# Expert-choice encoder layer: the next expert's rows picked and gathered at an earlier place, and the first expert's choice in another order

## The chip, the cores and the metric

The kernel runs on one NeuronCore of a Trainium2 chip. The metric is the device time of one launch in microseconds. Engines in the profile: PE is TensorE, PEld its weight loads, DVE VectorE, ACT ScalarE, POOL GpSimd, SP SyncE. Two queues of DMA matter here: plain loads and stores that SP issues, and the indirect ones (gather and scatter by row index) that POOL issues.

## The reference

One transformer layer, applied with the same weights to a request of 512 tokens (prompt) and one of 2048 tokens (sample), all float32, width 1024:

```
h = x + W_out @ concat[DiffAttn(n), BandGQA(n)],   n = RMSNorm(x)
y = h + ExpertChoiceSwiGLU(RMSNorm(h))

aff = softmax(xt @ w_router)                 # 16 experts
gates, idx = top_k(aff.T, C)                 # C = 2 T / 16: 256 sample rows, 64 prompt rows
xe = xt[idx]
h  = silu(xe @ w_gate[e]) * (xe @ w_up[e])
ye = (h @ w_down[e]) * gates
y.at[idx].add(ye)
```

Each expert picks its rows, so every one of the 16 experts handles 320 rows (256 of the sample, 64 of the prompt).

## The kernel before, in words

The first 1600 us compute projections, attention and the output projection. The output projection runs over 20 blocks of 128 tokens (0 to 15 sample, 16 to 19 prompt). In block b, `outproj` makes the two halves of h, `norm2` (L1411) stores h and its normalised rows, and the block before is transposed (`split_n`, L1388) and given its router logits and softmax (`router`, `router_2`). Work that doesn't belong to the projection is hung in with `at(t, f)` and fires on the t-th `tick`, of which there are about 18 in a block. In the blocks 17 to 19 this carries `choose`, the search for the first expert's threshold, a step at each `slot()` (places in `SLOTS`, L1470); its last steps write the one-hots of the chosen rows (`onehot_s`, L1308) and `pick` the rows.

`pick` (L1315) multiplies the one-hots with row numbers and gates on TensorE (L1329), copies the result (L1332), makes the indices `idx` (L1333) and gates (L1334) on DVE, and then issues three gathers on POOL (L1342): two of 128 sample rows from `n2s_d`, one of 128 rows (the 64 prompt rows twice) from `n2p_d`, 4 KB a row.

Then come the experts, e = 0 to 15. The float32 products run as three fp32r products of high and low parts, so every weight chunk (128 x 2048) is loaded by SP (`w_load`), split into high (ACT, L160) and low (DVE, L161) parts (`w_split`), and used two steps later. `gate_up` has 8 steps f; each makes 24 matmuls for the gate half, then calls `mid()`, then 24 for the up half. In `mid` the kernel does its side work in this order: the split of sums, the weight split and next load, the one-hots of the next expert y (f = 0), and its `pick` (f = 1 from expert 3 on, f = 2 for expert 2). From f = 4 on, `turn` transposes the gathered rows of y, two of eight steps in each f, the first in `mid` of f = 4 (L1584): this needs all three gathers.

From expert 2 on `down_blocks` (L1671) makes the down projection and ends with the scatters, which add into the output in DRAM (L1810): the second sample group `ys[1]`, the prompt rows in two halves into the same rows of `out_p` (`scatter_p`, so that the second half waits until the first has landed), and the first sample group `ys[0]`. POOL runs its instructions in order, so the gathers of the next `pick` stand behind these four. On POOL there are then only the three small sums per f from f = 4 on (L1636 to L1638).

Of the kernel before, what the change touches and what calls it, by code (L numbers as in the profile page):

```python
# [23 lines left out]
NB = NS + NP  # L24
T = NB * P
HEADS = 4
E = 16
# [80 lines left out]
def hybrid_encoder_kernel(tc, a, out_s, out_p):  # L108
# [11 lines left out]
    with ctx:  # L120
# [54 lines left out]
        with ExitStack() as st:  # L175
# [160 lines left out]
            Z, R, X = {}, {}, {}  # L336
# [1023 lines left out]
        with ExitStack() as st:  # L1360
# [106 lines left out]
                    split_wo_l(1, h, k, nc.vector)  # L1467
            split_w(wrh[:, :, 0, :], wrh[:, :, 1, :], wrr)

            SLOTS = (2, 7, 12, 17), (4, 9, 14), (1, 6, 11, 14, 16, 17)  # L1470
            gens = []

            def slot():
                if gens:
                    try:
                        next(gens[0])
                    except StopIteration:
                        gens.pop(0)
# [4 lines left out]
            for b in range(NB):  # L1483
                if b + 2 < NB:
                    MX[b + 2] = load_mx(b + 2)
                if b + 1 < NB:
                    load_res(b + 1)
                if b == 0:
                    for j in range(HEADS * NP):
                        at(14 + 18 * j, lambda j=j: Prompt(0, j // NP, j % NP).start())  # L1490
                    for h in range(2, HEADS):
                        at(72 * h - 50, load_prompt, h)
                if b == NS + 1:
                    rest.close()
                    wsp = pool(ctx, "wsE", 3, side="right")
                if b >= 1:
                    if slow(b - 1):
                        at(12, split_n, b - 1)
                    t = 15 if slow(b - 1) else 13
                    at(t, router, b - 1)  # L1500
                    at(t + 2, router_2, b - 1)
                    if b < NS:
                        at(t + 7, router_3, b - 1)
                    if b == NS:
                        gens.append(first_sample(X[0]))
                        parts = gate_parts(affs, auxs, NS, "s")
                        at(17, router_3, b - 1)
                        at(17, slot)
                if b > NS:
                    at(1, router_3, b - 2) if b > NS + 1 else None  # L1510
                    for t in SLOTS[b - NS - 1]:
                        at(t, slot)
                    at(9, next, parts, None)
                    at(14, next, parts, None)
                if b == 2:
                    at(3, places, auxs, NS)
                    at(9, places, auxp, NP)
                if NS < b < NB - 1:
                    for i in range(4):
                        at(1 + 4 * i, w_split, i)  # L1520
                if b == 0:
                    tick(8)
                else:
                    outproj(b, 0)
                if b >= 1 and not slow(b - 1):
                    split_n(b - 1)
                tick(1)
                if b + 1 < NB:
                    MT[b + 1] = split_m(MX[b + 1])
                tick(1)  # L1530
                outproj(b, 1)
                norm2(b)
                if b == 1:
                    w_load()
                    w_load()
            while gens:
                slot()

        stay.close()

# [6 lines left out]
        with ExitStack() as st:  # L1547
# [123 lines left out]
            def down_blocks(x):  # L1671
# [69 lines left out]
                p = bank("gu1")  # L1741
                product(p, 5, "22b")
                added(y[2][1], q, 2, y[2][1])
                scatter_p(x, x.ys[2])
                added(y[0][1], p, 0, y[0][1])
                scatter(x.idx[:, 0:1], x.ys[0], out_s)
                w_split()
                w_load()

# [64 lines left out]
                for gi in range(2):  # L1814
                    scatter(x.idx[:, gi:gi + 1], x.ys[gi], out_s)

            def scatter_p(x, y):
                for hf in range(2):
                    scatter(x.idx[:CP, 2:3], y[hf * CP:(hf + 1) * CP, :], out_p)

            def last_block(x, y):
# [69 lines left out]
            for e in range(1, E):  # L1891
# [10 lines left out]
                for f in range(FC):  # L1902
                    def mid():
                        if y is not None and f >= 4:
                            turn(y, 2 * (f - 4))
                        if e < 2:
                            w_split()
                            w_load()
                        else:
                            if f:  # L1910
                                split_sums(x, f - 1)
                            if f < 6:
                                w_split()
                            else:
                                split_block(x, ("11", "21")[f - 6])
                            if f < 4:
                                w_load()
                        if y is not None and f == 0:
                            onehot_s(y)
                            onehot_p(y)  # L1920
                        if y is not None and f == (1 if e > 2 else 2):
                            pick(y, 0, 3)
                            if e == 2:
                                scatter_p(X[0], X[0].yp)
                        for n in {3: ("11",), 4: ("12", "22"), 5: ("21",)}.get(f, ()) if e >= 2 else ():
                            load_block(x, n)
# [67 lines left out]
```

## Time and profile before

| | |
|---|---|
| time, median of 3 runs | 3185.86 us (3182.30 to 3187.32) |
| the profiled execution | 3189.75 us, its span 3188.0 us |
| TensorE busy | 3045.8 us, 96% |
| VectorE, ScalarE, GpSimd busy | 2349.1, 1680.5, 1208.9 us |
| mean granted clock of TensorE | 0.989 |
| DMA | 448.26 MB, 141 GB/s over the span |

An expert takes about 88 us from expert 3 on. A row of a timeline gives an instruction's start and length, and the idle time of its engine just before it with what ended that idle time. "Landing" of a DMA is the time from its start on the queue until its completion is seen. Engines other than TensorE idle a good deal; that costs nothing unless TensorE waits for them.

### The profile page before, as it was taken

To read this page: it belongs to the slowest core of one execution; us is meant where nothing else is said; L and a number is where in the kernel's file an instruction comes from. 1 tells how busy PE (TensorE), PEld (TensorE's weight loads), DVE (VectorE), ACT (ScalarE), POOL (GpSimd) and SP (SyncE) were. 2 spreads that over 40 slices of the span, in tenths; PEclk is the share of its full clock that TensorE was granted. 3 is DMA by queue.
4 is the path that set the end of the run, shared out by engine and by line. 5 is a ranking of instruction groups with operands and counts; after the bars stand their busy time and mean duration, and the time that the engine had idled before them with its cause. 6 is when DMAs were issued, how large, how long until landed. Compare 5 with 4: busy or idle time off the path is not lost. (4 is left out here: it accounts for less than half of the span.)

```text
span 3188.0 us, 50336 instructions
## 1 busy us (share of the span) xinstructions
PE 3045.8 (96%) x18996; PEld 2717.8 (85%) x18996; DVE 2349.1 (74%) x4297; ACT 1680.5 (53%) x3199; POOL 1208.9 (38%) x1116
## 2 busy tenths in 40 slices
PE   7998999998999999999997999999999999999997
PEld 5887888886888888888876899999999989999996
DVE  6887777777787788854566656778877767777876
ACT  4333666656777777743333454445555444444553
POOL 3665655554556556632234302122212122222211
PEclk9999999999999999999998999999999999999998
DMA  6664111136030301055533667665555556666553
GB/s 215 179 178 153 57 46 47 56 75 154 22 88 21 87 21 59 28 172 159 156 120 132 196 207 231 198 198 172 177 191 182 192 180 204 212 198 197 170 177 117
DMA packets 169138, 448.26 MB, mean 141 GB/s; under 512 B 15232, under 2 KB 91648, under 8 KB 138560
## 3 DMA queue, kind: packets, MB, share of 16 engines
q1 hardware_dynamic: 152608, 388.68, 37.4%
q0 software_dynamic: 16288, 56.37, 7.7%
q8 instruction: 150, 2.46, 0.3%
q14 instruction: 92, 0.75, 0.1%
HBM read 359.54 MB, written 82.84 MB: 139 GB/s over the span
## 5 line engine op out<-in xcount | busy, mean ns | idle before, releaser
L167 PE MATMUL gu<-xeh,whi 128*128 128x320 f32 (+1 forms) x2048 | 641.8, 313 | 0.0
L169 PE MATMUL gu<-xeh,wlo 128*128 128x320 f32 (+1 forms) x2048 | 631.0, 308 | 0.7 <-DVE wlo L161 0.7
L168 PE MATMUL gu<-xel,whi 128*128 128x320 f32 (+1 forms) x2048 | 630.7, 308 | 0.0
L161 DVE TENSOR_TENSOR wlo<-wraw,whi 128x2048 fp32r<-128x2048 f32 x180 | 412.8, 2296 | 163.5 <-ACT whi L160 163.5
L160 ACT ACTIVATE whi<-wraw 128x2048 fp32r<-128x2048 f32 x180 | 343.2, 1911 | 106.5 <-DMA wraw<-w_gu 50.4
L167 PEld LDWEIGHTS gu<-xeh,whi 128*128 128x128 f32 x2048 | 387.5, 189 | 2.9 <-issue 2.3
L168 PEld LDWEIGHTS gu<-xel,whi 128*128 128x128 f32 x2048 | 386.9, 189 | 0.6
L169 PEld LDWEIGHTS gu<-xeh,wlo 128*128 128x128 f32 x2048 | 386.1, 189 | 0.9 <-DVE wlo L161 0.9
L907 DVE TENSOR_REDUCE cmx<-s 128x1 f32<-128x1024 f32 x256 | 309.4, 1220 | 63.5 <-PE s L895 61.0
L1810 POOL DMA_INDIRECT out_dram<-y,idx x62 | 125.3, 2021 | 582.7 <-DVE y L1692 337.2
L918 ACT ACTIVATE p<-s,cmx 128x1024 f32<-128x1024 f32 x256 | 285.1, 1115 | 81.4 <-DVE cmx L909 78.0
L895 PE MATMUL s<-kd,qd 128*128 128x512 f32 x1024 | 295.3, 416 | 23.8 <-ACT p L918 22.2
L960 PE MATMUL cpo<-vd,aT 128*128 128x128 f32 x2048 | 267.3, 276 | 0.7 <-DVE co L965 0.7
L960 PEld LDWEIGHTS cpo<-vd,aT 128*128 128x128 f32 x2048 | 250.8, 192 | 8.8 <-ACT aT L953 4.6
L167 PE MATMUL z<-w,xh 128*128 128x512 f32 (+1 forms) x624 | 241.1, 386 | 11.7 <-ACT w L163 6.8
L940 POOL TENSOR_SCALAR p<-p,cr 128x1280 f32<-128x1280 f32 (+1 forms) x80 | 144.1, 1802 | 228.6 <-DVE cr L930 190.4
L169 PE MATMUL z<-w,xl 128*128 128x512 f32 (+1 forms) x624 | 229.8, 368 | 0.3 <-POOL xl L692 0.3
L895 PEld LDWEIGHTS s<-kd,qd 128*128 128x128 f32 x1024 | 177.9, 191 | 61.2 <-ACT p L918 35.6
L168 PE MATMUL z<-w,xh 128*128 128x512 f32 (+1 forms) x624 | 229.2, 367 | 0.5 <-DVE w L164 0.5
L953 ACT ACTIVATE aT<-cpt 128x512 f32<-128x512 f32 x272 | 161.8, 595 | 118.3 <-PE cpt L948 114.5
L1636 POOL TENSOR_TENSOR s<-hr,s 128x128 f32<-128x128 f32 x56 | 26.5, 474 | 486.8 <-DVE hr L1604 486.8
L942 POOL TENSOR_TENSOR p<-p,p 128x1280 f32<-128x1280 f32 (+1 forms) x80 | 207.3, 2591 | 6.6
(416 smaller groups left out, 7172.7 us busy)
## 6 DMA issues: line engine op xcount, KB each, us to landing
wraw<-w_gu SPq DMA_DIRECT2D x136, 1024.0 KB, 6.8
b<-w_dn SPq DMA_DIRECT2D x42, 1024.0 KB, 9.1
wraw<-w_dn SPq DMA_DIRECT2D x40, 1024.0 KB, 4.9
xr<-xT SPq DMA_DIRECT2D x40, 512.0 KB, 4.8
kd<-k_d SPq DMA_DIRECT2D x16, 1024.0 KB, 16.5
xtok<-x SPq DMA_DIRECT2D x20, 512.0 KB, 5.0
q_d<-hl SPq DMA_DIRECT2D x20, 512.0 KB, 3.5
k_d<-hl SPq DMA_DIRECT2D x20, 512.0 KB, 3.4
```

What stands on the lines that cost most here:

```text
L160: nc.scalar.activation(hi, raw, AF.Copy)
L161: nc.vector.tensor_sub(lo, raw, hi.bitcast(F32))
L167: nc.tensor.matmul(out, xh, wh, start=start, stop=False)
L168: nc.tensor.matmul(out, xh, wl, start=False, stop=False)
L169: nc.tensor.matmul(out, xl, wh, start=False, stop=stop)
L895: nc.tensor.matmul(s, q, u.keys(c, hl, k0), start=(hl == 0), stop=(hl == 1))
L907: nc.vector.tensor_reduce(m[:, j % 2:j % 2 + 1], u.S[j], axis=AX, op=OP.max)
L918: nc.scalar.activation(u.pr[c][:, half * 1024:(half + 1) * 1024], u.S.pop(j), AF.Exp, bias=u.mx[:, c, 2:], scale=SCALE, accum_out=u.sm[:, ...
L940: nc.gpsimd.tensor_scalar(p1, p1, u.r[:, 1:2], 1.0, op0=OP.mult, op1=OP.mult)
L942: nc.gpsimd.tensor_tensor(p0, p0, p1, op=OP.add)
L953: nc.scalar.activation(u.aT[:, 4 * g:4 * g + 4, :], u.pt, AF.Copy)
L960: nc.tensor.matmul(u.po, u.aT[:, kb, :], u.values(kb), start=(kb == 0), stop=(kb == u.nb - 1))
```

## The change

1. Experts 3 to 14: in `mid` of f = 1, `pick` of the next expert now stands ahead of the weight split and load (in the changed file at L1922). The scatters of the expert before are cut in two: `down_blocks` issues `ys[1]` and the first prompt half; the second prompt half and `ys[0]` (`late_scatters`) are issued only behind that pick's gathers. For the experts 14 and 15 all scatters stay at the end of `down_blocks`.
2. The first expert's choice: the transposes, router and softmax of block 18 leave block 19's projection and come after the pick of the first expert; the last `slot()` of the search, which writes the one-hots, is called after the projection instead of at tick 17.

```diff
@@ -1467,7 +1467,7 @@
                     split_wo_l(1, h, k, nc.vector)
             split_w(wrh[:, :, 0, :], wrh[:, :, 1, :], wrr)
 
-            SLOTS = (2, 7, 12, 17), (4, 9, 14), (1, 6, 11, 14, 16, 17)
+            SLOTS = (2, 7, 12, 17), (4, 9, 14), (1, 6, 11, 14, 16)
             gens = []
 
             def slot():
@@ -1493,7 +1493,7 @@
                 if b == NS + 1:
                     rest.close()
                     wsp = pool(ctx, "wsE", 3, side="right")
-                if b >= 1:
+                if 1 <= b < NB - 1:
                     if slow(b - 1):
                         at(12, split_n, b - 1)
                     t = 15 if slow(b - 1) else 13
@@ -1529,12 +1529,17 @@
                     MT[b + 1] = split_m(MX[b + 1])
                 tick(1)
                 outproj(b, 1)
+                if b == NB - 1:
+                    slot()
                 norm2(b)
                 if b == 1:
                     w_load()
                     w_load()
             while gens:
                 slot()
+            split_n(NB - 2)
+            router(NB - 2)
+            router_2(NB - 2)
 
         stay.close()
 
@@ -1741,9 +1746,10 @@
                 p = bank("gu1")
                 product(p, 5, "22b")
                 added(y[2][1], q, 2, y[2][1])
-                scatter_p(x, x.ys[2])
+                scatter_p(x, x.ys[2], (0,))
                 added(y[0][1], p, 0, y[0][1])
-                scatter(x.idx[:, 0:1], x.ys[0], out_s)
+                if x.e > E - 3:
+                    late_scatters(x)
                 w_split()
                 w_load()
 
@@ -1814,8 +1820,12 @@
                 for gi in range(2):
                     scatter(x.idx[:, gi:gi + 1], x.ys[gi], out_s)
 
-            def scatter_p(x, y):
-                for hf in range(2):
+            def late_scatters(x):
+                scatter_p(x, x.ys[2], (1,))
+                scatter(x.idx[:, 0:1], x.ys[0], out_s)
+
+            def scatter_p(x, y, halves=(0, 1)):
+                for hf in halves:
                     scatter(x.idx[:CP, 2:3], y[hf * CP:(hf + 1) * CP, :], out_p)
 
             def last_block(x, y):
@@ -1909,6 +1919,9 @@
                         else:
                             if f:
                                 split_sums(x, f - 1)
+                            if y is not None and f == 1 and e > 2:
+                                pick(y, 0, 3)
+                                late_scatters(X[e - 1])
                             if f < 6:
                                 w_split()
                             else:
@@ -1918,7 +1931,7 @@
                         if y is not None and f == 0:
                             onehot_s(y)
                             onehot_p(y)
-                        if y is not None and f == (1 if e > 2 else 2):
+                        if y is not None and f == 2 and e <= 2:
                             pick(y, 0, 3)
                             if e == 2:
                                 scatter_p(X[0], X[0].yp)
```

On POOL, at the border of experts 3 and 4 (`y_2151x` are the output rows of expert 3, `xe_` the gathered rows of expert 5), before:

```order
L1810 DMA out_dram<-y_21511,idx 2048x1024
L1810 DMA out_dram<-y_21512,idx 512x1024 x2
L1810 DMA out_dram<-y_21510,idx 2048x1024
L1342 DMA xe_21864<-n2s_d,idx 128x1024
L1342 DMA xe_21866<-n2s_d,idx 128x1024
L1342 DMA xe_21868<-n2p_d,idx 128x1024
L1636 TENSOR_TENSOR s<-hr,s_21702 128x128
```

and now (lines of the changed file are 5 or 6 higher):

```order
L1816 DMA out_dram<-y_21511,idx 2048x1024
L1816 DMA out_dram<-y_21512,idx 512x1024
L1342 DMA xe_21856<-n2s_d,idx 128x1024
L1342 DMA xe_21858<-n2s_d,idx 128x1024
L1342 DMA xe_21860<-n2p_d,idx 128x1024
L1816 DMA out_dram<-y_21512,idx 512x1024
L1816 DMA out_dram<-y_21510,idx 2048x1024
L1641 TENSOR_TENSOR s<-hr,s_21700 128x128
```

The second prompt half and the first sample group have moved behind the three gathers.

On DVE in the half-step f = 1 of expert 4 (`ax`, `idx` and `gate` are the pick's, `wlo` the weight split's low part), before:

```order
L1640 TENSOR_TENSOR hp<-hr,hp 128x64
L161 TENSOR_TENSOR wlo<-wraw,whi 128x2048
L1332 COPY ax<-cnt 128x15
L1333 SCALAR_TENSOR_TENSOR idx<-ax 128x3
L1334 TENSOR_REDUCE gate<-ax 128x3
L1604 TENSOR_TENSOR hr<-hr,gu_21870 128x320
```

and now:

```order
L1645 TENSOR_TENSOR hp<-hr,hp 128x64
L1332 COPY ax<-cnt 128x15
L1333 SCALAR_TENSOR_TENSOR idx<-ax 128x3
L1334 TENSOR_REDUCE gate<-ax 128x3
L161 TENSOR_TENSOR wlo<-wraw,whi 128x2048
L1609 TENSOR_TENSOR hr<-hr,gu_21870 128x320
```

The three instructions of the pick have moved ahead of the split.

On TensorE around the first expert's choice, from the last matmul of the pick on (`pt_1784x` and `pt_1785x` take the transposes of block 19, `n_177xx`; `pt_17886` is the first of the first expert's gathered rows), before:

```order
L1329 MATMUL s<-auxs,wraw 128x5
L1828 MATMUL pt_17848<-ident,n_17775 128x128 x4
L1828 MATMUL pt_17855<-ident,n_17775 128x128 x4
L1459 MATMUL pt<-ident,many 112x128
L1433 MATMUL pt<-xeh,wrh 32x128 x8
L1433 MATMUL pt<-xel,wrh 32x128 x8
L1570 MATMUL pt_17886<-ident,wraw 128x128 x4
```

and now (`n_17599` is block 18):

```order
L1329 MATMUL s<-auxs,wraw 128x5
L1392 MATMUL dpt<-ident,n_17599 128x128 x8
L1433 MATMUL cpo<-nth,wrh 32x128 x8
L1433 MATMUL cpo<-ntl,wrh 32x128 x8
L1442 MATMUL cpo<-ident,lt 128x32
L1838 MATMUL pt_17848<-ident,n_17731 128x128 x4
L1838 MATMUL pt_17855<-ident,n_17731 128x128 x4
L1459 MATMUL pt<-ident,many 112x128
L1433 MATMUL pt<-xeh,wrh 32x128 x8
L1433 MATMUL pt<-xel,wrh 32x128 x8
L1575 MATMUL pt_17886<-ident,wraw 128x128 x4
```

The rows from L1392 to L1442 stood in the last output projection before and now stand in the gap after the pick.

## Rows read from the trace of the kernel before

**Rows 1.** The page, busy time of an engine (share of the span) and its instructions.

```profile
PE 3045.8 (96%) x18996; PEld 2717.8 (85%) x18996; DVE 2349.1 (74%) x4297; ACT 1680.5 (53%) x3199; POOL 1208.9 (38%) x1116
```

**Rows 2.** The waits of TensorE (PE) from 2000 to 3180 us, all lines of the answer: who waited for what: us in total, times, longest.

```profile
PE pt L1584 <- DMA xe<-n2p_d,idx: 17.9, 12, 3.6
PE pt L1584 <- DMA xe<-n2s_d,idx: 1.5, 1, 1.5
```

**Rows 3.** TensorE's timeline at the transposes of the next expert's rows, expert 7 (2410) and expert 9 (2586 to 2594): start us, us, engine, line, operation, times; in brackets the idle time before it and what ended it.

```profile
2410.74 0.33 PE L1584 MATMUL pt<-ident,xe 128*128 128x128 f32 x1 [1.76 <-DMA xe<-n2p_d,idx]
...
2586.41 0.33 PE L1584 MATMUL pt<-ident,xe 128*128 128x128 f32 x1 [1.50 <-DMA xe<-n2s_d,idx]
2590.35 0.48 PE L1584 MATMUL pt<-ident,xe 128*128 128x128 f32 x1 [3.61 <-DMA xe<-n2p_d,idx]
...
2593.56 0.47 PE L169 MATMUL gu<-xeh,wlo 128*128 128x320 f32 x1
```

**Rows 4.** Busy time by stretch (from:to and length in us; PE, PEld, DVE, ACT, POOL busy; then TensorE's granted clock, the DMA engines' mean busy share, GB/s).

```profile
1710.00:1715.00 5.00, 1.66 (x23) 1.57 (x23) 2.30 (x7) 1.15 (x3) 1.20 (x2) 0.50 0.36 140
...
2390.00:2395.00 5.00, 5.00 (x36) 5.00 (x36) 3.63 (x8) 2.22 (x6) 4.31 (x3) 1.00 0.59 90
...
2405.00:2410.00 5.00, 3.98 (x28) 3.74 (x26) 1.12 (x4) 0.66 (x3) 0.00 (x0) 1.00 1.02 423
...
2591.00:2592.00 1.00, 1.00 (x6) 1.00 (x5) 0.64 (x2) 1.00 (x3) 0.00 (x0) 0.50 1.04 434
```

**Rows 5.** POOL's timeline, expert 7 (2379 to 2417) and expert 9 (2573); columns as in rows 3. L1810 is a scatter, L1342 a gather, L1636 the first of the three sums.

```profile
2379.05 2.62 POOL L1810 DMA_INDIRECT out_dram<-y,idx  x1 [0.30 <-issue]
2390.08 1.42 POOL L1810 DMA_INDIRECT out_dram<-y,idx  x1 [8.41 <-DMA out_dram<-y,idx]
2391.81 2.56 POOL L1810 DMA_INDIRECT out_dram<-y,idx  x1 [0.30 <-issue]
2394.67 1.00 POOL L1342 DMA_INDIRECT xe<-n2s_d,idx  x1 [0.30 <-issue]
...
2397.24 2.06 POOL L1342 DMA_INDIRECT xe<-n2p_d,idx  x1 [0.30 <-issue]
2416.67 0.46 POOL L1636 TENSOR_TENSOR s<-hr,s 128x128 f32<-128x128 f32 x1 [17.37 <-DVE hr L1604]
...
2573.30 1.00 POOL L1342 DMA_INDIRECT xe<-n2s_d,idx  x1 [0.30 <-issue]
```

**Rows 6.** The chain of waits, in expert 7 (2397 and 2411) and expert 9 (2575 and 2590): start us, us, what.

```profile
2397.24 13.45 DMA xe<-n2p_d,idx
...
2411.07 0.15 PE gu L167
...
2575.88 14.43 DMA xe<-n2p_d,idx
...
2590.83 0.27 PE gu L167
```

**Rows 7.** Timelines of DVE (VectorE) and, at 2567.33, of ACT (ScalarE): the half-step in which the next expert's rows are picked, expert 7 (2388 to 2393) and expert 9 (2564 to 2569).

```profile
2388.17 0.22 DVE L1640 TENSOR_TENSOR hp<-hr,hp 128x64 fp32r<-128x64 f32 x1
2390.64 2.29 DVE L161 TENSOR_TENSOR wlo<-wraw,whi 128x2048 fp32r<-128x2048 f32 x1 [2.25 <-ACT whi L160]
2392.85 0.17 DVE L1332 COPY ax<-cnt 128x15 f32<-128x15 f32 x1
2393.05 0.16 DVE L1333 SCALAR_TENSOR_TENSOR idx<-ax 128x3 int32<-128x3 f32 x1
...
2564.18 0.21 DVE L1640 TENSOR_TENSOR hp<-hr,hp 128x64 fp32r<-128x64 f32 x1
...
2567.33 1.91 ACT L160 ACTIVATE whi<-wraw 128x2048 fp32r<-128x2048 f32 x1 [3.25 <-DMA wraw<-w_gu]
...
2569.27 2.29 DVE L161 TENSOR_TENSOR wlo<-wraw,whi 128x2048 fp32r<-128x2048 f32 x1 [4.88 <-ACT whi L160]
```

**Rows 8.** TensorE's timeline around the first expert's choice. L1392 are transposes and L1433 router matmuls; L169 is the last matmul of the last output projection, L1828 the last block's transposes, L1570 those of the first expert's gathered rows.

```profile
1696.70 1.03 PE L1392 MATMUL dpt<-ident,n 128*128 128x128 f32 x8
...
1699.76 0.65 PE L1433 MATMUL cpo<-nth,wrh 128*32 128x128 f32 x8
...
1705.00 0.39 PE L169 MATMUL do<-wo,mtl 128*128 128x512 f32 x1
...
1713.85 1.97 PE L1828 MATMUL pt<-ident,n 128*128 128x128 f32 x8 [3.35 <-DVE n L1424]
...
1717.53 1.05 PE L1433 MATMUL pt<-xel,wrh 128*32 128x128 f32 x8
...
1722.85 3.46 PE L1570 MATMUL pt<-ident,wraw 128*128 128x128 f32 x15 [0.80 <-DMA wraw<-n2s_d,idx]
```

**Rows 9.** Timelines of DVE and, at 1714.35, of POOL in the same stretch. L1308 are the one-hots of the first expert, L1409 the addition of the projection, L1424 the last normalisation's product.

```profile
1706.61 3.22 DVE L1308 TENSOR_SCALAR wraw<-iota_s,slots 128x256 bf16<-128x256 bf16 x16
1709.74 0.68 DVE L1409 TENSOR_TENSOR xres<-do,xres 128x512 f32<-128x512 f32 x1
...
1712.51 1.28 DVE L1424 SCALAR_TENSOR_TENSOR n<-xres,dst,ffn_g 128x1024 f32<-128x1024 f32 x1 [0.66 <-POOL dst L155]
...
1714.35 1.11 POOL L1342 DMA_INDIRECT wraw<-n2s_d,idx  x1 [1.88 <-DVE fold L1867]
```

**Rows 10.** The page's DMA issues: what, queue, operation, times, size of one, median us from issue to landing.

```profile
wraw<-w_gu SPq DMA_DIRECT2D x136, 1024.0 KB, 6.8
```

## The prediction

> **What bounds the kernel now.** I read the busy times first: TensorE works 3045.8 of 3188.0 us [rows 1], so it sets the time, and only its idle time and its slow clock can be won back. Then I listed what TensorE waits for in the part of the experts 3 to 15 (2000 to 3180 us). The list has two lines, both at the transposes of the next expert's gathered rows (L1584): 12 waits of 17.9 us in total for the third gather and one of 1.5 us for an earlier one [rows 2]; one wait each in the experts 3 to 14, plus a second in expert 9. Nothing else stops TensorE there. So I looked at two of these waits, in expert 7 (1.76 us, a common size) and in expert 9 (1.50 and 3.61 us, the largest) [rows 3], and followed each back. The chain of waits says gather: the third gather of expert 7 takes 13.45 us from its start on the queue to landing, that of expert 9 14.43 us [rows 6]. Why it starts so late is in POOL's timeline: the gathers stand behind the second prompt scatter, which waits 8.41 us for the first one to land (both add into the same rows), and behind the scatter after it [rows 5]. DVE's timeline has a second reason: the row indices come at 2393.05, behind the split of the next weight chunk, which itself waited for that chunk to arrive [rows 7]. Last I read the stretch around 1700 us, where the first expert's rows are chosen [rows 8, 9].
>
> **Part 1: pick ahead of the split, gathers ahead of two scatters (experts 3 to 14).** It adds and removes no work; three DVE instructions, three gathers and two scatters change places.
> In expert 7, DVE is done with the half-step before at 2388.4 (2388.17 + 0.22) and then idles until 2390.64, waiting for ScalarE [rows 7]. The pick's copy and its index instruction took 2392.85 to 2393.21 [rows 7], so they fit into that hole: indices at about 2388.8, the gate behind them within another 0.1, and the split isn't delayed. POOL is free from 2381.7 (2379.05 + 2.62) [rows 5]. The first gather then goes out at about 2389.1 instead of 2394.67, 5.6 us earlier, the third at 2391.7 instead of 2397.24. With the landing time of before, 13.45 us [rows 6], the third is there at 2405.1. TensorE came to the transposes at 2409.0 (2410.74 less 1.76) [rows 3]: 3.9 us to spare. In the worse case, with each issue as long as the longest in these rows (2.06 us) and 14.43 us to land, it is 2408.2, still in time. In expert 9 DVE is free at 2564.4, the first gather went out only at 2573.30 [rows 5, 7]: it moves by about 8.2 us, and the waits were 5.1 us together. So I take the whole of the waits: 17.9 + 1.5 = **19.4 us** [rows 2].
> In expert 9 the long wait also cost clock. The granted clock fell to 0.50, the 1.2 GHz level, after TensorE had stood still from 2586.7 to 2590.35 [rows 3, 4], and the matmuls behind it came every 0.27 us where those of expert 7 came every 0.15 [rows 6], about 12 of them until 2593.56 [rows 3]: 12 x 0.12 = **1.4 us**, gone with the wait. Bounds for the part: 20.8 us at most, as rows 2 hold no other idle time of TensorE; at least nothing, if the gathers don't land earlier.
> What is put behind: the second prompt scatter and the sample scatter go out at about 2394 and 2396 instead of 2390.08 and 2391.81. POOL's next work is at 2416.67 [rows 5], so nobody on POOL waits; the experts 14 and 15 keep the old order, so the program's last scatter doesn't move. I cost this at nothing; without that cover of 18 us POOL would hold up the next sums.
> Nothing is late next in the chain of TensorE: the weight chunk split in this half-step is ready at 2392.93 (2390.64 + 2.29) and TensorE wants it at about 2398.4 (an estimate: 2409.0 less three half-steps of 24 matmuls at 0.147). In expert 9 the same margin is 2571.56 against about 2574.3, 2.7 us [rows 3, 7].
> The Trainium skill (DMA: Bandwidth & Descriptors, "Anatomy of one DMA — SWDGE (gpsimd) path") prices a DMA issued by GpSimd at about 2.0 us plus its bytes at 436 GB/s, which for 128 rows of 4 KB would be 3.2 us: by it the third gather would have landed at 2400.4 already before, TensorE would not have waited, and this part would give 0. The row with 13.45 us [rows 6] speaks against it, and the measured number decides: in this stretch the 16 DMA engines are full, share 1.02 at 423 GB/s from 2405 to 2410 [rows 4].
>
> **Part 2: the first expert's choice.** Block 18's transposes, its router matmuls and the seven small DVE instructions of its softmax leave the last output projection and go behind the pick. Out of TensorE's way before the projection's end go 8 transposes (1.03 us), 16 router matmuls (two groups like the one of 0.65 us) and a small transpose [rows 8], some 2.0 us less their overlap with what follows: it ends at about 1703.4 instead of 1705.4. The addition of the projection (0.68 us) now stands ahead of the one-hots, so these run from about 1704.1 to 1707.3 (3.22 us) [rows 9] instead of from 1706.61 to 1709.8; the last normalisation, and behind it the indices, come 4.4 us earlier (the product on DVE at about 1708.1, 0.8 us after the one-hots, instead of 1712.51); the first gather goes out at 1709.9 instead of 1714.35 [rows 9] and the second lands at 1718.4, as 8.5 us lay between the first issue and the transposes at 1722.85 [rows 8, 9]. The moved work is not free: TensorE does it in the gap at 1.2 GHz (granted 0.50 from 1710 to 1715 [rows 4]), so 2.0 us for transposes and 2.1 us for router matmuls (lengths of the like groups at 1713.85 and 1717.53 [rows 8]), plus the splits and the softmax between. By my sum that pushes the last block's transposes back to about 1713.8, where they were, and TensorE is through with them at 1718.6 to 1719.2, as before (1717.53 + 1.05). The gather was the later one; now both are level. Gain: from 1722.85 to about 1719.3, **3.5 us**. No row shows the moved chain at its new place; bounds are 4.4 us (all that the gather gains) and a loss of 1 us (the chain 4.5 us longer than I put it, about its own length again). I take 3.5, nearest to the rows of the same groups.
>
> **Sum.** 19.4 + 1.4 + 3.5 = 24.3 us off the profiled execution's 3189.75: **3165 us**. That execution is 3.9 us above the median of the runs (3185.86). Expert 9's long stall (3.8 us over the 1.3 us of the other eleven, and its 1.4 us of clock) may well be what sets it apart; such a stall goes with the rest, so the time after is the same whether or not a run has it.
>
> **Rivals.**
> *The gathers are slowed in their new place.* They now run beside the end of the first scatters and beside two weight loads. If they took 18.5 us instead of 13.45, the third would land at 2410.2 and 1.2 us of wait would stay. In eight of the twelve experts that is 10 us, and the time is **3175**. Against it: 3.9 us of margin, and from 2390 to 2395 the DMA engines moved only 90 GB/s [rows 4].
> *The transfers are bound by bandwidth, not by their start.* The engines may be so full from the scatters on that the third gather lands at 2410 whatever its issue. Then only part 2 is left: **3186**, no change that can be told. For it: the share of 1.02 from 2405 to 2410; against it: the 90 GB/s from 2390 to 2395, where the gathers now run.
> *Slower: the weights come late.* The gathers' 1.5 MB take 3.7 us at 423 GB/s [rows 4] and now fall upon the weight chunks. Up to 2.7 us (expert 9) or 5.5 us (expert 7) of delay cost nothing [rows 7]; from there each us costs 12. To end 6.4 us slower the chunk would have to come some 8 us late in every expert: **3195**. A load takes 6.8 us on the median [rows 10] and would have to double, so I hold this for unlikely.
> The Trainium skill (the same page, "Queues, rings and completion order") says that each DMA engine serves the queue rows in turn, packet by packet; by that rule the gathers would take half of the engines from the weight loads beside them, which is this rival's mechanism. The arrival of expert 9's chunk, for which ScalarE waited 3.25 us just after scatters on the other queue [rows 7], agrees with it.
> That the change doesn't do what it says I leave out: the instruction order on DVE and POOL shows it.
>
> **How the numbers follow.** Chances: forecast 0.76, slowed gathers 0.11, bandwidth 0.07, weights late 0.06. About 0.2%, 6.4 us, is what a measurement of this kernel can tell from no change. The first two are faster by more than that, so faster 0.87, same 0.07, slower 0.06. Range: low end 3165.4 less 3.9 (if the profile itself costs that), less 0.9 (part 2 at its bound), less 3.6 (the runs' spread below the median, 3185.86 to 3182.30): 3157; high end 3176, which takes in the slowed gathers.
>
> **What would show it.** Right: no wait of TensorE for a gather from 2000 us on; first gathers of an expert about 5 to 8 us earlier against the half-step, indices ahead of the split on DVE; the second prompt scatter behind them; in the first expert the transposes of the gathered rows near 1719. Wrong: waits of TensorE at L1584's counterpart that stay near 1 us, a new wait for the split weights (wlo), or gathers whose landing grows by what their start gained.

## The result, and the profile after

| | before | after |
|---|---|---|
| time, median of 4 runs each | 3186.59 us (3182.30 to 3187.90) | 3162.48 us (3161.92 to 3166.45) |
| ratio, 95% interval | | 0.9929, 0.9912 to 0.9947 |
| the profiled execution | 3189.75 us, span 3188.0 us | 3162.34 us, span 3160.6 us |
| mean granted clock of TensorE | 0.989 | 0.991 |

The change makes the kernel faster by 24.1 us between the medians and by 27.4 us between the two profiled executions. Forecast: 3165 us (3157 to 3176), 24.3 us between the executions.

The page of the changed kernel, busy time of an engine, answers to [rows 1]: TensorE does the same number of matmuls in nearly the same busy time, so the time came out of its idle stretches.

```profile
PE 3041.0 (96%) x18996; PEld 2714.9 (86%) x18996; DVE 2348.3 (74%) x4297; ACT 1679.1 (53%) x3199; POOL 1210.6 (38%) x1116
```

The waits of TensorE from 2000 to 3180 us, asked as in [rows 2], have no line left. The same question for its weight loads (PEld; the gathered rows are what a transpose loads as weights), first in the kernel before:

```profile
PEld pt L1584 <- DMA xe<-n2p_d,idx: 20.7, 12, 3.8
PEld pt L1584 <- DVE xel L1586: 1.8, 10, 0.2
PEld pt L1584 <- DMA xe<-n2s_d,idx: 1.8, 1, 1.8
```

and in the changed kernel:

```profile
PEld pt L1589 <- DVE xel L1591: 2.2, 12, 0.2
```

The two lines that name a gather are gone. They held 20.7 + 1.8 = 22.5 us, where the matmul's own lines [rows 2] held 19.4: at each wait the load stands still a little longer than the matmul behind it.

POOL's timeline in expert 7 of the changed kernel, which answers to [rows 5] (L1816 is a scatter, L1342 a gather, L1641 the first sum):

```profile
2369.29 2.67 POOL L1816 DMA_INDIRECT out_dram<-y,idx  x1 [0.30 <-issue]
2379.62 1.00 POOL L1342 DMA_INDIRECT xe<-n2s_d,idx  x1 [7.66 <-issue]
2380.92 0.97 POOL L1342 DMA_INDIRECT xe<-n2s_d,idx  x1 [0.30 <-issue]
2382.19 2.91 POOL L1342 DMA_INDIRECT xe<-n2p_d,idx  x1 [0.30 <-issue]
2385.41 1.49 POOL L1816 DMA_INDIRECT out_dram<-y,idx  x1 [0.30 <-issue]
2387.20 1.57 POOL L1816 DMA_INDIRECT out_dram<-y,idx  x1 [0.30 <-issue]
2404.99 0.46 POOL L1641 TENSOR_TENSOR s<-hr,s 128x128 f32<-128x128 f32 x1 [16.21 <-DVE hr L1609]
```

Take the start of the first prompt half as the zero of an expert: 2379.05 before, 2369.29 here. The first gather starts at 10.33 instead of 15.62, the third at 12.90 instead of 18.19. POOL still idles 16.21 us before its next sum, so the two late scatters hold up nobody.

DVE and TensorE in the same expert of the changed kernel, answering to [rows 7] and [rows 3]: the indices stand right behind the half-step before, the weight split after them waits for ScalarE as it did, and the transposes start with no wait.

```profile
2378.33 0.21 DVE L1645 TENSOR_TENSOR hp<-hr,hp 128x64 fp32r<-128x64 f32 x1
2378.47 0.16 DVE L1332 COPY ax<-cnt 128x15 f32<-128x15 f32 x1
2378.66 0.17 DVE L1333 SCALAR_TENSOR_TENSOR idx<-ax 128x3 int32<-128x3 f32 x1
2382.00 2.29 DVE L161 TENSOR_TENSOR wlo<-wraw,whi 128x2048 fp32r<-128x2048 f32 x1 [3.10 <-ACT whi L160]
...
2398.90 0.49 PE L1589 MATMUL pt<-ident,xe 128*128 128x128 f32 x3
```

The row that I had not forecast is in the DMA issues from 2000 to 3050 us (last column: median us to landing), in the kernel before

```profile
out_dram<-y,idx POOLq DMA_INDIRECT x48, 8.0
xe<-n2s_d,idx POOLq DMA_INDIRECT x24, 12.2
xe<-n2p_d,idx POOLq DMA_INDIRECT x12, 13.4
```

and in the changed one:

```profile
out_dram<-y,idx POOLq DMA_INDIRECT x48, 10.1
xe<-n2s_d,idx POOLq DMA_INDIRECT x24, 5.1
xe<-n2p_d,idx POOLq DMA_INDIRECT x12, 8.0
```

The prediction moved the gathers forward and kept their landing time; in fact the landing time fell from 12.2 and 13.4 us to 5.1 and 8.0, and the scatters took 2 us longer. So either move alone might have been enough, and the experiments take them apart.

For the first expert, DVE's last addition of block 18's projection (L1409, two in a block) in the kernel before and in the changed one is a common mark,

```profile
1687.36 0.68 DVE L1409 TENSOR_TENSOR xres<-do,xres 128x512 f32<-128x512 f32 x1
```

```profile
1686.28 0.68 DVE L1409 TENSOR_TENSOR xres<-do,xres 128x512 f32<-128x512 f32 x1
...
1706.39 1.92 PE L1392 MATMUL dpt<-ident,n 128*128 128x128 f32 x8
1708.40 1.06 ACT L1417 ACTIVATE n<-xres 128x1024 f32<-128x1024 f32 x1 [18.04 <-PE dpt L1392]
1712.24 1.11 POOL L1342 DMA_INDIRECT wraw<-n2s_d,idx  x1 [1.88 <-DVE gate L1334]
1720.67 3.21 PE L1575 MATMUL pt<-ident,wraw 128*128 128x128 f32 x15 [0.71 <-DMA wraw<-n2s_d,idx]
```

From the mark to the second group of transposes (1722.85 in [rows 8]) it was 35.49 us and is 34.39: 1.1 us gained, not 3.5. ScalarE's row says why: block 19's normalisation (L1417) waited until block 18's transposes (L1392), now behind the pick, had read their rows. Both use the one buffer `n2` (the pool `tk` has one of each name).

### The profile page after: what moved, and what is told of

Same layout as the page of the kernel before. It is cut to its first block, busy times and chain, and to the rows that moved or that the text cites. A ratio compares the mean times of both kernels' runs of the same rounds, so it can differ in the third digit from the quotient of the medians.

```text
span 3160.6 us, 50326 instructions
## 1 busy us (share of the span) xinstructions
PE 3041.0 (96%) x18996; PEld 2714.9 (86%) x18996; DVE 2348.3 (74%) x4297; ACT 1679.1 (53%) x3199; POOL 1210.6 (38%) x1116
## 5 line engine op out<-in xcount | busy, mean ns | idle before, releaser
L169 PE MATMUL gu<-xeh,wlo 128*128 128x320 f32 (+1 forms) x2048 | 629.5, 307 | 0.7 <-DVE wlo L161 0.7
L169 PEld LDWEIGHTS gu<-xeh,wlo 128*128 128x128 f32 x2048 | 384.8, 188 | 0.9 <-DVE wlo L161 0.9
L1816 POOL DMA_INDIRECT out_dram<-y,idx x62 | 122.7, 1979 | 487.5 <-DVE y L1697 337.5
L169 PE MATMUL z<-w,xl 128*128 128x512 f32 (+1 forms) x624 | 229.7, 368 | 0.3 <-POOL xl L692 0.3
L1641 POOL TENSOR_TENSOR s<-hr,s 128x128 f32<-128x128 f32 x56 | 26.5, 473 | 461.5 <-DVE hr L1609 461.5
```

The lines of the kernel that those rows point to most:

```text
L169: nc.tensor.matmul(out, xl, wh, start=False, stop=stop)
```

## The experiments

All were timed in 5 or more runs, beside the kernel before on the same chip. Three chips gave the kernel before 3181.43 us (experiments 1 to 3), 3179.82 us (4, 5 and the first of 7) and 3181.3 us (6 and the second of 7), so the ratio counts.

**1. Each part alone.** First the changed kernel without its first-expert part:

```diff
-            SLOTS = (2, 7, 12, 17), (4, 9, 14), (1, 6, 11, 14, 16)
+            SLOTS = (2, 7, 12, 17), (4, 9, 14), (1, 6, 11, 14, 16, 17)
...
-                if 1 <= b < NB - 1:
+                if b >= 1:
...
-                if b == NB - 1:
-                    slot()
...
-            split_n(NB - 2)
-            router(NB - 2)
-            router_2(NB - 2)
```

> The changed kernel with its first-expert part undone: only the earlier pick and the two scatters behind the gathers are left. Theory A (nearly the whole gain is the removed gather waits of the experts 3 to 14): 22 to 23 us under the kernel before, about 3164 us, no wait of TensorE for a gather after 2000 us. Rival (the first-expert part carries its forecast 3.5 us): about 3166 us, 20 to 21 us under. The transposes of the first expert's gathered rows should start near 1722 us as in the kernel before.

Measured: 3164.64 us (3162.26 to 3165.69), ratio 0.9945 (0.9932 to 0.9958), no wait for a gather after 2000 us; from the mark to the second transposes 35.46 us, as before. The time is that of theory A; the gain, 16.8 us, is less than either theory had, as the kernel before is 5 us faster here than in the first measurement, from which both were reckoned. Then the kernel before with that part alone (the same lines, the other way round).

> The kernel before with only the first-expert part. Forecast: 3.5 us under the kernel before. My reading of the trace of the changed kernel: block 19's normalisation has to wait for block 18's transposes because both use one n2 buffer, so the part gives 1 to 2 us: about 3185. All 12 to 13 waits for the third gather stay, some 17 to 20 us in sum, with landings of 12 to 13 us on the median.

Measured: 3178.65 us (3169.49 to 3184.11), ratio 0.9990 (0.9980 to 1.0000), waits for the third gather of 14.3 us in 9, landings of 11.4 us; mark to second transposes 34.38 us. Nearly the whole gain is the first part's. The second gives 1.1 us by the mark; the runs can't tell that from nothing or from the forecast 3.5 us, as their interval is 0 to 6.4 us.

**2. The pick early, the scatters as before.** The changed kernel with

```diff
-                if x.e > E - 3:
-                    late_scatters(x)
+                late_scatters(x)
...
                                 pick(y, 0, 3)
-                                late_scatters(X[e - 1])
```

> The changed kernel with all four scatters back at the end of down_blocks; the pick stays ahead of the weight split. Theory A (POOL's order holds the gathers: they stand behind the second prompt half, which waits for the first to land): indices are ready 4 us earlier and wait; first gather in expert 7 still near 2394 us on the axis of the kernel before, landing 12 to 13 us, the 12 waits stay at 15 to 20 us in sum, time 19 to 22 us above the changed kernel. Rival (the late indices on DVE were what held the gathers): waits fall by more than half, time within 8 us of the changed kernel.

Measured: 3183.51 us (3172.95 to 3189.25), ratio 1.0006 (0.9995 to 1.0017): no gain, and 19 us above the first kernel of experiment 1 on the same chip. The profiled execution was among the fastest (3173.45 us), hence the smaller sum in the waits of TensorE from 2000 to 3180 us:

```profile
PE pt L1589 <- DMA xe<-n2p_d,idx: 8.7, 7, 2.2
PE pt L1589 <- DMA xe<-n2s_d,idx: 0.9, 2, 0.5
```

and in expert 7 the gathers stand behind POOL's wait for the first prompt half, while DVE had the indices before it (rows in order of time):

```profile
2375.10 2.63 POOL L1815 DMA_INDIRECT out_dram<-y,idx  x1 [0.30 <-issue]
...
2384.46 0.17 DVE L1333 SCALAR_TENSOR_TENSOR idx<-ax 128x3 int32<-128x3 f32 x1
...
2385.23 1.42 POOL L1815 DMA_INDIRECT out_dram<-y,idx  x1 [7.50 <-DMA out_dram<-y,idx]
2386.96 2.63 POOL L1815 DMA_INDIRECT out_dram<-y,idx  x1 [0.30 <-issue]
2389.90 0.99 POOL L1342 DMA_INDIRECT xe<-n2s_d,idx  x1 [0.30 <-issue]
```

The indices were there at 2384.63, 5.3 us before the first gather started. The early pick alone buys nothing.

**3. The pick late, the scatters behind the gathers.** The changed kernel with `pick` and `late_scatters` moved back behind the weight split and load:

```diff
-                            if y is not None and f == 1 and e > 2:
-                                pick(y, 0, 3)
-                                late_scatters(X[e - 1])
...
-                        if y is not None and f == 2 and e <= 2:
+                        if y is not None and f == (1 if e > 2 else 2):
                             pick(y, 0, 3)
+                            if e > 2:
+                                late_scatters(X[e - 1])
```

> The changed kernel with the pick back behind the weight split and load, and the two scatters still behind the gathers. The indices come near 2393 (axis of the kernel before), so the first gather goes out only about 1.1 us earlier than before. Theory A (what counts is the start; a gather takes its 12 to 13 us to land): about 0.5 us of wait stays in each of 12 experts and more in some, 5 to 9 us in sum, time 6 to 9 us above the changed kernel. Theory B (a gather lands in 5 to 8 us once the accumulating scatters no longer go ahead of it on the queue): no wait stays, time within 2 us of the changed kernel, landings of 5 us (sample) and 8 us (prompt) on the median.

Measured: 3161.66 us (3160.72 to 3165.00), ratio 0.9942 (0.9929 to 0.9955), no wait left: the whole gain without the early pick. The starts alone don't explain it. In expert 7 the third gather starts here at 16.71 after the first prompt half (2367.40), 1.5 us earlier than before:

```profile
2384.11 2.73 POOL L1342 DMA_INDIRECT xe<-n2p_d,idx  x1 [0.30 <-issue]
```

The waits there were 1.5 us on average (17.9 in 12), but 3.6 at the largest. This profile has no landing times of the gathers; what their queue did is in the profile's DMA queues (packets, MB, share of the 16 engines; q0 is POOL's, q1 SP's). From the start of the third gather to 8.9 us later, 2384.11 to 2393 us,

```profile
q0 software_dynamic: 468, 1.72, 61.8%
q1 hardware_dynamic: 187, 1.27, 39.2%
```

(more than the bytes of the three gathers) and in the kernel before from 2397.24 until that gather had landed 13.4 us later:

```profile
q1 hardware_dynamic: 385, 2.79, 51.1%
q0 software_dynamic: 576, 2.10, 50.4%
```

Three gathers are 1.57 MB. Before, the queue had 0.53 MB more to move in that time: the first sample group's scatter, issued at 2391.81, of which nothing had moved when the third gather was issued. The gathers stood behind it. The Trainium skill (DMA: Bandwidth & Descriptors, "Two DMAs through the same engine are not ordered") says that descriptors of one queue start in order; these rows agree with it. The plain loads moved more as well, 2.79 against 1.27 MB, so these rows alone don't part the two causes.

**4. Which of the two scatters?** Experiment 3, with only the second prompt half behind the gathers:

```diff
                 if x.e > E - 3:
-                    late_scatters(x)
+                    scatter_p(x, x.ys[2], (1,))
+                scatter(x.idx[:, 0:1], x.ys[0], out_s)
...
             def late_scatters(x):
                 scatter_p(x, x.ys[2], (1,))
-                scatter(x.idx[:, 0:1], x.ys[0], out_s)
```

> Late pick (behind the weight split); of the two scatters only the second prompt half stands behind the gathers, the first sample group goes out ahead of them again as soon as the earlier sample group has landed, some 2 to 4 us ahead of the first gather. Theory B1 (a gather must get past the scatters that are still unfinished in its queue): the gathers stand behind 0.5 MB of scatter, landings between 8 and 12 us, part of the waits comes back, 3 to 10 us, time 3165 to 3173. Theory B2 (what held the gathers was POOL, which stood still for the first prompt half to land): no wait comes back, time within 2 us of the changed kernel.

Measured: 3162.91 us (3159.84 to 3163.74), ratio 0.9943 (0.9930 to 0.9956), no wait. Then with only the first sample group behind them:

```diff
-                scatter_p(x, x.ys[2], (0,))
+                scatter_p(x, x.ys[2])
...
             def late_scatters(x):
-                scatter_p(x, x.ys[2], (1,))
                 scatter(x.idx[:, 0:1], x.ys[0], out_s)
```

> Late pick; of the two scatters only the first sample group stands behind the gathers, the second prompt half waits on POOL for the first one again, 7.5 to 8.4 us, and goes out some 2 to 3 us ahead of the first gather. Theory B1: only 0.26 MB of scatter is ahead of the gathers, landings 7 to 10 us, few waits, 0 to 4 us in sum, time 3161 to 3166. Theory B2: POOL stands still as in the kernel before but is free when the indices come, so the gathers start nearly as early as with both scatters behind them: the same, 3161 to 3163. A third theory (the accumulating prompt rows block the queue until the first half has landed): landings of 12 us, waits of 10 us or more, 3172 or more.

Measured: 3165.43 us (3162.24 to 3167.68), ratio 0.9953 (0.9939 to 0.9966), no wait. The gathers' landings in the two, first with the prompt half late, then with the sample group late:

```profile
xe<-n2s_d,idx POOLq DMA_INDIRECT x24, 6.1
xe<-n2p_d,idx POOLq DMA_INDIRECT x12, 10.0
```

```profile
xe<-n2s_d,idx POOLq DMA_INDIRECT x24, 7.0
xe<-n2p_d,idx POOLq DMA_INDIRECT x12, 11.1
```

Either scatter alone may stay ahead. With the sample group ahead, the third gather starts at 17.0 after the first prompt half, nearly where it does in experiment 3, and lands in 10.0 us, where in experiment 3 the bytes of all three, if they move in order, were through in some 8.9: by this one scatter costs about 1 us of landing, not the 5 that the changed kernel won. Landings grow as B1 said, but the waits do not come back, as B2 said: I had priced 3 to 10 us of wait for what is only a smaller margin.

**5. How much room is left?** Experiment 3 with the pick at f = 2 for every expert:

```diff
-                        if y is not None and f == (1 if e > 2 else 2):
+                        if y is not None and f == 2:
```

> Both scatters behind the gathers, but pick and gathers one half-step pair later (f = 2 for all experts, 7.7 us later), so that they run among the extra loads of w_dn. Theory B (a third gather takes 8 us when no scatter is ahead of it on its queue): the third gather of expert 7 would land 2.7 us after TensorE is ready for it, 2 to 3 us of wait in each of 12 experts, time about 3190 to 3195. Theory C (it was the plain loads beside the gathers that made them take 13 us in the kernel before, 3.1 MB then against 1.2 to 2.0 MB in the faster kernels): landings of 13 us again, 7 to 8 us of wait in each expert, 3245 or more.

Measured: 3215.64 us (3204.78 to 3228.07), ratio 1.0110 (1.0085 to 1.0135). That is 52.7 us above the first kernel of experiment 4, timed beside it, or 4.4 us in each of 12 experts, between the two theories. Its DMA issues, and in expert 7 TensorE's wait (the third gather started at 2416.97) and the stretch behind it, with a granted clock of 0.50:

```profile
xe<-n2s_d,idx POOLq DMA_INDIRECT x23, 6.0
xe<-n2p_d,idx POOLq DMA_INDIRECT x11, 11.1
```

```profile
2428.12 0.33 PE L1589 MATMUL pt<-ident,xe 128*128 128x128 f32 x1 [4.32 <-DMA xe<-n2p_d,idx]
...
2429.00:2432.00 3.00, 3.00 (x13) 3.00 (x12) 1.87 (x3) 2.57 (x3) 0.00 (x0) 0.50 1.01 309
```

No scatter is ahead here, yet the third gather needs 11.1 us, not 8: between its start and 2428.1 the plain loads moved 2.38 MB beside it, where in the changed kernel they moved 0.96 MB in the 8.0 us behind 2382.19. So the scatters are not the only cause; that the loads are the other is read from these rows and wasn't tested by itself. Part of the 4.4 us is clock: nine such slow stretches stand behind transposes of this kernel, two in the kernel before. Put together, for expert 7, counted from the start of the first prompt half (TensorE is ready for the third gather at 2408.98 - 2379.05 = 29.9; "there at" is the start and the median landing together; the waits are those of TensorE from 2000 to 3180 us in all experts):

| kernel | scatters moved behind | third gather starts | landing, median | there at | waits, us |
|---|---|---|---|---|---|
| before | none | 18.2 | 13.4 | 31.6 | 19.4 |
| early pick alone | none | 19.4 | 10.9 | 30.3 | 9.6 |
| late pick | sample group | 17.3 | 11.1 | 28.4 | 0 |
| late pick | prompt half | 17.0 | 10.0 | 27.0 | 0 |
| the changed kernel | both | 12.9 | 8.0 | 20.9 | 0 |
| pick at f = 2 | both | 23.1 | 11.1 | 34.2 | 40.4 in 9 |

**6. The smallest change.** The kernel before, and in it only this (`scatter_p` gets the argument `halves` as in the change):

```diff
-                scatter_p(x, x.ys[2])
+                scatter_p(x, x.ys[2], (0, 1) if x.e > E - 3 else (0,))
...
                             pick(y, 0, 3)
+                            if e > 2:
+                                scatter_p(X[e - 1], X[e - 1].ys[2], (1,))
```

> The kernel before with one edit: in the experts 3 to 14 the second prompt half is issued behind the gathers instead of ahead of them. No earlier pick, no other scatter moved, first expert as before. If one scatter fewer ahead of the gathers (and POOL not standing still for it) is enough, no wait of TensorE for a gather is left, landings near 6 us (sample) and 10 us (prompt) on the median, time that of the changed kernel without its first-expert part: 0.9945 of the kernel before, 3163 to 3165 us. If the earlier pick has a share in the gain, 2 us or more above that, with waits left.

Measured, beside the changed kernel run again on that chip:

> The changed kernel itself, on the same chip as the two other kernels of this group: 0.993 to 0.995 of the kernel before, 3160 to 3164 us, no wait of TensorE for a gather after 2000 us.

3163.54 us (3160.64 to 3165.23), ratio 0.9943 (0.9926 to 0.9961), against 3162.98 (3160.94 to 3165.80), 0.9942 (0.9925 to 0.9960). No wait in either. One scatter moved gives the whole gain as far as the runs can tell.

**7. The first expert, mended.** The changed kernel with block 18's transposes and split ahead of block 19's normalisation:

```diff
                 if b == NB - 1:
                     slot()
+                    split_n(b - 1)
                 norm2(b)
...
-            split_n(NB - 2)
```

> The changed kernel with block 18's transposes and their split moved from behind the first expert's pick to ahead of block 19's normalisation. If the one n2 buffer is what holds that normalisation (ScalarE waited until 1708.40 for the transposes at 1706.39), ScalarE starts it near 1705, the first gather goes out 1.5 to 2.5 us earlier than 1712.24 and the transposes of the gathered rows start near 1718.5: time 1 to 2 us under the changed kernel, about 3161. Rival (the chain over the router of block 18 on TensorE is the longer one): the gather goes out earlier and the transposes stay at 1720.7, time as the changed kernel.

Measured: 3162.43 us (3159.67 to 3162.84), ratio 0.9944 (0.9932 to 0.9957). From the mark to the second transposes 32.57 us instead of 34.39: 1.8 us gained where it was expected, while that execution had been 3.6 us later at the mark (1689.87), which the edit doesn't touch. In time it is not to be told from the changed kernel (0.9942 on another chip). Going on, the pick inside the normalisation; `split_n` calls `between` behind its transposes, `norm2` behind its power, and `finish` makes the remaining steps of the search, the pick among them:

```diff
                     slot()
-                norm2(b)
+                    split_n(b - 1, lambda: norm2(b, finish))
+                else:
+                    norm2(b)
...
-            while gens:
-                slot()
-            split_n(NB - 2)
```

> The changed kernel with the first expert's pick placed inside block 19's normalisation: block 18's transposes first, then the square and its power, the pick, then the product and block 18's split. Counted from the last addition of block 18's projection, the second transposes of the first expert's gathered rows start 47.3 us later in the kernel before, 44.8 in the changed kernel, 43.0 with the split ahead of the normalisation. If the indices are what the gather waits for, the first gather goes out 2 us earlier again and this distance is 41 us: time 3158 to 3160 at the median, 3 to 4 us under the changed kernel on the same chip. Rival (the router of block 18 and the last block's transposes on TensorE, now later, become the longer chain): the distance stays at 43 and the time at 1 to 2 us under the changed kernel.

Measured: 3161.70 us (3159.34 to 3165.01), ratio 0.9938 (0.9920 to 0.9956). By the mark

```profile
1687.94 0.68 DVE L1410 TENSOR_TENSOR xres<-do,xres 128x512 f32<-128x512 f32 x1
...
1708.91 2.01 POOL L1342 DMA_INDIRECT wraw<-n2s_d,idx  x1 [0.67 <-DVE gate L1334]
...
1719.02 3.46 PE L1580 MATMUL pt<-ident,wraw 128*128 128x128 f32 x15 [0.77 <-DMA wraw<-n2s_d,idx]
```

it is 31.08 us, 3.3 below the changed kernel. Counted as the expectation did, from 1676.10 (block 18's first addition, which it calls the last), it is 42.9, the rival's number; but that stretch holds an episode of slow clock, which the kernel before and this one had and the changed one had not (below), worth 1.4 us, and without it the distance is 41.5. No kernel here is shown to beat the changed one in time: 3161.7 against 3163.0 on the same chip, with runs that spread over 5 to 6 us.

## Why the prediction was right, step by step

The 27.4 us between the profiled executions, cut at rows of the traces:

| stretch | us | forecast |
|---|---|---|
| to the mark (1687.36 to 1686.28) | 1.1 | 0 |
| first expert's choice (35.49 to 34.39) | 1.1 | 3.5 |
| from there to the first transposes L1584 (332.35 to 331.33) | 1.0 | 0 |
| from these to the last ones (2055.2 to 3059.3; now 2052.0 to 3032.2) | 23.9 | 20.8 |
| the rest | 0.3 | 0 |

**The waits.** Right in place: TensorE's waits for gathers go whole. The term of 20.8 us, which was also given as the most that could be won, was 3.1 us too small, for two reasons. It took the matmuls' rows, 19.4, where the weight loads' rows have 22.5; in expert 3 the last matmul ahead of the transposes and the first behind them (2055.04 and 2057.62) lie 2.19 us further apart than with no wait, which is the weight load's 2.21 and not the matmul's 1.97. And it priced the slow clock of expert 9 alone. Expert 3's wait was followed by one too:

```profile
2057.53 0.33 PE L1584 MATMUL pt<-ident,xe 128*128 128x128 f32 x1 [1.97 <-DMA xe<-n2p_d,idx]
...
2058.00:2061.00 3.00, 3.00 (x14) 3.00 (x13) 1.50 (x3) 2.98 (x4) 0.00 (x0) 0.51 0.94 396
```

Twelve matmuls took 3.20 us there, from 2058.19 to 2061.39, instead of 1.76: another 1.4 us. That makes 22.5 + 1.4 + 1.4 = 25.3, more than the 23.9 of the stretch, because the changed kernel loses 1 us elsewhere. In expert 5 the pick's matmuls run behind one-hots that come later; before and now:

```profile
2210.89 0.96 PE L1329 MATMUL cnt<-auxs,oh 128*128 128x5 bf16 x32
```

```profile
2202.83 1.78 PE L1329 MATMUL cnt<-auxs,oh 128*128 128x5 bf16 x32
```

No wait row shows this, as the engine counts as busy. DVE's one-hots stood behind a weight split for whose chunk ScalarE had waited 3.16 us, before 1.94. The first-expert part alone has such a delay too (1.57 us in experiment 1), with the gathers in their old place, so it isn't shown to be the gathers' doing. The last 0.4 us are left open.

**The way there.** The first gather starts 5.3 us earlier (forecast 5.6), with 13.45 us to land as assumed the third would have been in time by 3.6 us. But the landing was not the constant that I took it for: 8.0 instead of 13.4, so it is there 9 us early. And the early pick, half of my explanation [rows 7], has no share: with the scatters in their old place it gives nothing (experiment 2), and without it the gain is whole (experiments 3, 6). The indices were late, as I read, but to no effect, since POOL came free later still: in expert 7 at 2394.37, the indices at 2393.21.

**Neighbours.** As forecast, nobody waits for the late scatters and TensorE has no row of waiting for the split weights; the scatters' own landing grew from 8.0 to 10.1 us at no cost.

**The first expert.** Up to the one-hots it went as forecast: they start 16.4 us behind the mark (1702.67), where 16.7 had been put. The step that failed is "the last normalisation, and behind it the indices, come 4.4 us earlier". I had followed queues and engines, not buffers: the normalisation writes `n2`, which the moved transposes still had to read. Counted from the mark, the first gather was to go out at 22.5 us (1709.9) and went out at 26.0, only 1.0 us earlier than before. Experiment 7 shows that this wait was it: with the transposes ahead of the normalisation, ScalarE starts it 4.6 us and POOL the gather 2.7 us earlier, and 1.8 us of that reach TensorE.

**The rivals.** The estimate of 3.2 us from the Trainium skill's formula (DMA: Bandwidth & Descriptors, "Anatomy of one DMA — SWDGE (gpsimd) path") did not hold for these gathers in any kernel: the shortest median of a gather was 5.1 us, and 7.8 for the third one. Gathers slowed in the new place: the reverse, they land sooner. Bandwidth as the bound: refuted at f = 1, since nothing waits; for f = 2 not excluded, as the landing is 11.1 us beside the loads of SP. Late weights: no wait of TensorE's for them, at most the delay in expert 5.

**The size.** That the forecast, 3165, lies 2.5 us from the measured median is in part luck. The first expert's term was 2.4 us too large and the waits' 3.1 us too small, which nearly cancel. On another chip the same change gave 0.9942 (0.9925 to 0.9960), 18 us. In groups of six runs or more, kernels with gather waits spread over 10 to 23 us, those without over 5 to 6. What is gained seems to depend on how late the gathers came in that execution: with waits of 19.4, 14.3 and 9.6 us the profiled ones took 3189.75, 3179.36 and 3173.45 us.

## What to carry to other kernels

Where one queue carries gathers and accumulating scatters, put what somebody waits for ahead of what nobody waits for, and don't carry a landing time along as a constant: in these runs it depended on what was unfinished ahead in the queue. Read a stop for weights from the weight loads' rows, and look for slow clock behind every stop, not only the longest. When two reasons for a late start stand side by side, only the later one counts; try each alone. Before moving work behind a step, look up which single buffers that step writes.

## What the runs showed of the hardware

Landing of a gather of 128 rows of 4 KB: 5.1 to 12.2 us on the median for the first two of three, 7.8 to 13.4 us for the third. It was shortest with both scatters moved behind, at f = 1; at f = 2, with both behind and 2.38 MB of plain loads beside it in expert 7, the third took 11.1 us.

The granted clock falls to the 1.2 GHz level after short stops, but not in every execution. After TensorE had stood 2.16 us until 1675.66 it was granted 0.50 from 1676 to 1679 in the kernel before, and 1.00 in the changed kernel after the same stop:

```profile
1676.00:1679.00 3.00, 3.00 (x10) 2.40 (x9) 2.93 (x6) 1.12 (x2) 3.00 (x3) 0.50 0.52 175
```

```profile
1676.00:1679.00 3.00, 3.00 (x21) 2.65 (x21) 2.93 (x4) 1.49 (x4) 3.00 (x3) 1.00 0.41 152
```

Neither goes with the edit (the smallest change had 1.00 there, the last experiment 0.56). From block 18's first addition to the mark the stretch is 1.4 us longer with it (11.84 against 10.42 us), more than the whole second part gave, and a reading of that part from a mark ahead of it would have been wrong by that.
